# Moving decode, set-up and the last block's projections in a two-layer hybrid decoder step

## The chip, the core and the metric

The kernel runs on one core of one Trainium2 chip. The time is device microseconds of that core for one whole execution: the prompt of 2048 tokens and eight sample tokens through two layers. Three runs are shown, and a profile of one execution.

## What is computed

Each layer normalises its input, makes one projection of width 3332 and feeds four token mixers of width 256, whose outputs, each through its own gate, are concatenated and projected back to 1024:

```python
hn = rms_norm(x, norm_w)
proj = hn @ w_in            # r_q r_k r_v r_g | g_q g_f g_i g_g | s_u s_g | m_z m_xbc m_dt
o_ret  = head_rms(retention(rq, rk, rv)) * silu(r_g)              # "A"
o_hgrn = head_rms(gated_recurrence(hq, hk, hv, log_f)) * silu(g_g) # "H"
gy = gelu(s5_scan(s_u) + s5_D * s_u)                               # "S"
o_s5 = gy * sigmoid(gy @ s5_glu_w + s5_glu_b) * silu(s_g)
o_m2 = rms(ssd(conv(m_xbc), m_dt) * silu(m_z))                     # "M"
x = x + concat(o_ret, o_hgrn, o_s5, o_m2) @ w_out
```

The same layers are applied to the prompt (states start at zero) and to the eight sample tokens (states are given); all new states are outputs. A final rms_norm ends both streams. All is float32.

## The kernel before

**Tiling.** The prompt goes in eight blocks of 512 tokens, four to a layer, in order; `blocks[0..3]` are layer 0, `blocks[4..7]` layer 1. In this document *step i* is the i-th pass of the main loop over blocks. A block's normalised input is held transposed in eight tiles `hn`, each as a rounded value and its remainder, so that each projection takes three matmul passes (L620, L625, L687). Weights come in slices `wr`, are split into `wh` on ScalarE and VectorE (L607/608, L680/681) and used at once. A projection is a Python generator that yields after every slice: 8 yields for a wide one (`gemm_wide`, 512 columns), 4 for a narrow one (`gemm`, 256 columns). Block i has A and H projections (16 yields each), M (12) and S (8), and an output projection (16 in two halves of 512 columns).

**Mixers.** `mix_A`, `mix_H`, `mix_S` and `mix_M` are generators too. `begin` puts one into a lane. After every yield of a projection, `tick` runs at most two mixers one step each (lanes m, s, a, h) and one step of the lanes d, e, f, p (decode and set-up). `yield n` in a mixer asks for n rounds of pause, cut to `most` (1 for the first block's A and H, else 9). `drain` runs named mixers to their end with no projection between. So the order of TensorE's instructions is written out by this code and kept (`manual_schedule` for PE); the other engines and the DMA queue on SP are ordered by the compiler's list scheduler, which follows program order shifted by `high_priority` offsets (set-up is put back by 100, decode by 50, projection weights ahead by 100).

**The main loop before.** Step i runs the A and H projections of block i, drains the mixers of block i-1, begins A and H of block i, runs the output projection of block i-1, then M and S projections with their mixers, and in between prepares the next block's `hn` (L581 to L584). In block 7 the order is: A, H, first half of block 6's output, S, M, second half of block 6's output, block 7's output.

**Set-up and decode.** `s5_setup` makes the S5 tables of a layer from its parameters (exponentials and sines by polynomial on VectorE, table pieces through DRAM: `gpad`, then L517, then `s5c`). Layer 0's is spawned at the start, layer 1's in step 1. `Dec` is the decode of the eight sample tokens: its projections ride on the block's (`dec_pass`, L630 and L694: the raw weights against eight columns), then `mix_A`, `mix_H`, `mix_M`, `mix_S` of `Dec` (L890 to L1070) on VectorE and SP, then its output. It is attached to blocks 0 and 4, the first of each layer.

**Buffers.** Pools have fixed counts: ten `half` tiles (128x512) and ten `big` tiles (128x1024) for all mixers, evictions, set-up and decode; eight `mx` tiles for the mixed outputs of a block. A mixer stores into an `mx` tile (`mix_store`, L722 to L725) only when the previous block's second output half has used it:

```python
def free(self, kt):
    return lambda: self.prev is None or self.prev.used > kt
```

S5's last part (L1458 to L1481) multiplies tables with states, transposes, applies Gelu (L1467), the GLU matmul (L1474), sigmoid (L1476) and the two products L1477 and L1478. Mamba's token tiles need masks from GpSimd (L1561), end in L1597/L1598 and L1637. The heads' post-processing of A and H ends in L736. The last block's output projection (`final` in `out_proj`) drains mixers between its slices:

```python
for g in gens[:2]:
    for k2 in range(3):
        drain(B.st["ahs"[k2]])
        next(g)
        yield
drain(B.st["m"])
```

In this kernel `E('g')`, `E('l')`, `E('s')`, `E('t')` stand for VectorE, `E('m')`, `E('f')`, `E('w')` for GpSimd.

Of the kernel before, what the change touches and what calls it, by code (L numbers as in the profile page):

```python
# [21 lines left out]
P = 128  # L22
D = 1024
KT = 8
# [89 lines left out]
def trunk_kernel(ctx: ExitStack, tc: tile.TileContext, A: dict):  # L114
# [229 lines left out]
    def sincos(sn, cn, hi, lo, shape):  # L344
        n = tmp_c(shape)
        r = tmp_c(shape)
# [19 lines left out]
    def s5_setup(L):  # L366
# [102 lines left out]
        for hf in range(2):  # L469
            yield 2  # L470
            ctz = half([P, 2, 4, 2, 16])
            gtile = half([P, 2, 8, 16])
# [197 lines left out]
    def gemm_wide(lhs, w, c0, evac, dec=None):  # L670
# [4 lines left out]
        def load(kt):  # L675
            with tc.high_priority(offset=WPRI):
                hl = whp.tile([P, 2, 520], F32R, name=nm("wh"), tag="wh")
                raw = wrp.tile([P, 520], F32, name=nm("wr"), tag="wr")
                nc.sync.dma_start(raw[:, 0:512], w[kt * P : (kt + 1) * P, c0 : c0 + 512])
# [5 lines left out]
        def t_pass(kt, tt):  # L685
            for pi, (a, c) in enumerate(((1, 0), (0, 1), (0, 0))):
                T.matmul(banks[tt], lhs[kt][:, a, tt * P : (tt + 1) * P], hls[kt][:, c, 0:512],  # L687
                         start=(kt == 0 and pi == 0), stop=(kt == KT - 1 and pi == 2))

        def dec_pass(kt):  # L690
            if dec is not None and kt % DW == DW - 1:
                for k in range(kt - DW + 1, kt + 1):
                    j = k % 4
                    T.matmul(dbank[32 * j : 32 * j + 8, :], dec[0]()[:, k, :], raws[k][:, 0:512], start=(k < 4), stop=(k >= 4))  # L694
# [43 lines left out]
    class Blk:  # L738
# [48 lines left out]
    class Dec:  # L787
# [209 lines left out]
        def mix_S(self):  # L997
            l, L = self.l, self.L
            gw = load_gw(L)
# [30 lines left out]
            y = half([P, 8, 2, 16])[0:8]  # L1030
# [11 lines left out]
            so = half([P, 2, P])[0:64]  # L1042
# [4 lines left out]
            db = half([P, 2, 256])[0:8]  # L1047
            us = half([P, 2, 256])[0:8]
            nc.sync.dma_start(us[:, 0], self.d["su"])
            nc.sync.dma_start(us[:, 1], self.d["sg"])  # L1050
            nc.sync.dma_start(db[:, 0], A["s5_D"][l].partition_broadcast(8))
            nc.sync.dma_start(db[:, 1], A["s5_glu_b"][l].partition_broadcast(8))
            V.tensor_tensor(db[:, 0], db[:, 0], us[:, 0], ALU.mult)
            V.tensor_tensor(yf, yf, db[:, 0], ALU.add)
# [6 lines left out]
            V.tensor_copy(gT, ps[:, 0:16].rearrange("p (k b) -> p k b", k=2))  # L1061
            yield 4
# [3 lines left out]
            V.tensor_tensor(db[:, 1], db[:, 1], ps[0:8, 0:256], ALU.add)  # L1066
            S.activation(db[:, 1], db[:, 1], AF.Sigmoid)
            V.tensor_tensor(yf, yf, db[:, 1], ALU.mult)
            V.tensor_tensor(yf, yf, us[:, 1], ALU.mult)
# [190 lines left out]
    def mix_H(L, B):  # L1260
# [124 lines left out]
    def mix_S(L, B):  # L1385
# [77 lines left out]
        for th in range(2):  # L1463
            ps = mbank()
            for t in range(4):
                T.transpose(ps[:, t * P : (t + 1) * P], Y[:, 7 - 4 * th - t, :], ident)
            S.activation(gy.rearrange("p h (j t) -> p t h j", t=8)[:, 4 * th : 4 * th + 4], ps.rearrange("p (t h j) -> p t h j", t=4, h=2),  # L1467
                         AF.Gelu_apprx_tanh)
        yield 2
        for mo in range(2):  # L1470
# [6 lines left out]
            E('g').tensor_tensor(sg, sg, B.sg[:, mo, :], ALU.mult)  # L1477
            V.tensor_tensor(sg, sg, gy[:, mo, :], ALU.mult)  # L1478
# [527 lines left out]
```

## Time and profile before

| | us |
|---|---|
| median of 3 runs | 2297.53 (2296.26 to 2297.86) |
| the profiled execution's own time | 2296.06 |
| span in its trace | 2294.3 |
| TensorE matmul busy | 2140.4 (93%) |
| VectorE busy | 1668.9 (73%) |
| ScalarE busy | 1037.3 (45%) |
| GpSimd busy | 236.4 (10%) |

Read the table together with the slices and stretches below: a share over the whole span hides where an engine waits. A busy TensorE may also run at the lower of its two clock levels (the column PEclk: 1.00 is the full level in all of the stretch).

### The profile page before, as it was taken

How to read it: one execution, taken by the hardware profiler on the slowest of the kernel's cores; microseconds unless marked ns; L12 is line 12 of the kernel's file. 1: busy time of each engine (PE TensorE's matmuls, PEld its weight loads, DVE VectorE, ACT ScalarE, POOL GpSimd, SP SyncE). 2: the span in 40 equal slices, each digit the busy share in tenths (PEclk: the TensorE clock that was granted, in tenths of full speed). 3: DMA queues.
4: the chain of work that ended last, by engine and by line, in shares of the span. 5: the costliest groups of instructions: out<-in, count | busy, mean ns of one | idle time of the engine just before them, and what ended most of it. 6: DMA issues, size and time to landing. Idle time of an engine off the chain costs nothing. (4 is left out here: it accounts for less than half of the span.)

```text
span 2294.3 us, 41082 instructions
## 1 busy us (share of the span) xinstructions
PE 2140.4 (93%) x15047; PEld 1732.4 (76%) x15047; DVE 1668.9 (73%) x4625; ACT 1037.3 (45%) x1893; POOL 236.4 (10%) x212
## 2 busy tenths in 40 slices
PE   7988898999999999999999999899999989999967
PEld 6767676778777887779777777676877778778856
DVE  6778885587957876397676798658875787647855
ACT  5334633346442464434543365334545345444423
POOL 1010102001022011101020000200101001110100
PEclk9998899999999999999999999999999999999988
DMA  6322466154533655243434246415454433533342
GB/s 190 91 58 71 155 167 155 50 147 127 168 101 109 159 161 165 68 138 87 146 116 134 82 134 180 145 61 177 116 159 122 127 105 100 163 87 109 121 134 84
DMA packets 265242, 284.94 MB, mean 124 GB/s; under 512 B 88848, under 2 KB 185760, under 8 KB 265040
## 3 DMA queue, kind: packets, MB, share of 16 engines
q1 hardware_dynamic: 265040, 282.31, 41.7%
q8 instruction: 118, 1.93, 0.3%
q14 instruction: 84, 0.69, 0.1%
HBM read 246.05 MB, written 31.99 MB: 121 GB/s over the span
## 5 line engine op out<-in xcount | busy, mean ns | idle before, releaser
L687 PE MATMUL gb<-wh,hn 128*128 128x512 f32 x2208 | 542.0, 401 | 3.7 <-DVE half L1626 3.6
L625 PE MATMUL gb<-hn,wh 128*128 128x512 f32 x1920 | 489.0, 408 | 7.0 <-DVE half L1118 7.0
L687 PEld LDWEIGHTS gb<-wh,hn 128*128 128x128 f32 x2208 | 411.3, 189 | 109.8 <-issue 13.8
L625 PEld LDWEIGHTS gb<-hn,wh 128*128 128x128 f32 x1920 | 361.7, 193 | 98.0 <-issue 11.9
L681 DVE TENSOR_TENSOR wh<-wr,wh 128x512 fp32r<-128x512 f32 x296 | 216.3, 735 | 273.2 <-ACT wh L680 271.7
L680 ACT CAST wh<-wr 128x512 fp32r<-128x512 f32 x296 | 183.4, 620 | 394.1 <-PE gb L687 193.4
L687 PE MATMUL gb<-wh,mx 128*128 128x512 f32 x1344 | 339.3, 405 | 7.4 <-DVE half L1700 6.9
L687 PEld LDWEIGHTS gb<-wh,mx 128*128 128x128 f32 x1344 | 250.0, 191 | 75.6 <-DVE half L1700 11.6
L607 ACT CAST wh<-wr 128x512 fp32r<-128x512 f32 (+1 forms) x248 | 152.2, 619 | 320.1 <-PE gb L625 95.9
L608 DVE TENSOR_TENSOR wh<-wr,wh 128x512 fp32r<-128x512 f32 (+1 forms) x248 | 183.2, 745 | 87.0 <-ACT wh L607 85.8
L620 PE MATMUL gb<-wh,hn 128*128 128x256 f32 (+1 forms) x1728 | 225.2, 291 | 2.1 <-DVE hn L556 1.1
L620 PEld LDWEIGHTS gb<-wh,hn 128*128 128x128 f32 x1728 | 217.6, 196 | 5.6 <-issue 2.6
L1561 POOL TENSOR_TENSOR half<-mats,m_lal 128x512 fp32r<-128x512 f32 x64 | 75.4, 1199 | 820.8 <-DVE m_lal L1555 311.0
L1317 DVE COPY_PREDICATED big<-lvl,mb 64x256 f32<-64x256 int32 x192 | 95.9, 538 | 2.7
L1284 ACT COPY zbH<-big 64x512 f32<-64x512 f32 x112 | 70.8, 632 | 46.7 <-PE mb L1293 39.4
L1499 DVE SCALAR_TENSOR_TENSOR big<-gb,vt,big 128x511 f32<-128x511 f32 (+2 forms) x96 | 71.1, 744 | 3.9 <-ACT big L1497 3.4
L1293 PE MATMUL mb<-zbH,big 128*64 128x64 f32 x1536 | 58.2, 232 | 5.2 <-ACT half L1165 3.5
L1293 PEld LDWEIGHTS mb<-zbH,big 128*64 128x64 f32 x1536 | 51.9, 145 | 14.5 <-issue 7.7
L1275 POOL TENSOR_TENSOR big<-mats,h_dg 128x1024 f32<-128x1024 f32 x16 | 30.6, 1932 | 282.3 <-DVE h_dg L1272 282.3
L1458 PE MATMUL mb<-big,big 128*64 128x128 f32 x512 | 40.7, 304 | 18.2 <-DMA big<-s5c 14.2
L620 PE MATMUL gb<-wh,mx 128*128 128x256 f32 x384 | 51.1, 298 | 4.6 <-DVE mx L1481 4.1
L620 PEld LDWEIGHTS gb<-wh,mx 128*128 128x128 f32 x384 | 50.0, 204 | 6.1 <-DVE mx L1481 4.9
(495 smaller groups left out, 3084.6 us busy)
## 6 DMA issues: line engine op xcount, KB each, us to landing
wr<-in_w_in SPq DMA_DIRECT2D x416, 256.0 KB
wr<-in_w_out SPq DMA_DIRECT2D x128, 256.0 KB
big<-s5c SPq DMA_DIRECT2D x64, 256.0 KB
xn<-xmid SPq DMA_DIRECT2D x32, 512.0 KB
xn<-in_x_prompt SPq DMA_DIRECT2D x24, 512.0 KB
big<-s5c SPq DMA_DIRECT2D x24, 512.0 KB
xmid<-half SPq DMA_DIRECT2D x44, 256.0 KB
half<-xmid SPq DMA_DIRECT2D x44, 256.0 KB
```

Of the source, the lines that this page charges most:

```text
L607: S.copy(hl[:, 0, :, :n], raw[:, :, :n])
L608: V.tensor_tensor(hl[:, 1, :, :n], raw[:, :, :n], hl[:, 0, :, :n].bitcast(F32), ALU.subtract)
L620: T.matmul(o, lhs[2 * ks[ki] + k][:, a, tt * P : (tt + 1) * P], hls[ki][:, c, k, :n], start=(ki == 0 and k == 0 and pi == 0 and tt % per = ...
L625: T.matmul(banks[i], hls[ki][:, a, k, i * P : (i + 1) * P], lhs[2 * ks[ki] + k][:, c, :], start=(ki == 0 and k == 0 and pi == 0), stop=(ki ...
L680: S.copy(hl[:, 0, 0:512], raw[:, 0:512])
L681: V.tensor_tensor(hl[:, 1, 0:512], raw[:, 0:512], hl[:, 0, 0:512].bitcast(F32), ALU.subtract)
L687: T.matmul(banks[tt], lhs[kt][:, a, tt * P : (tt + 1) * P], hls[kt][:, c, 0:512], start=(kt == 0 and pi == 0), stop=(kt == KT - 1 and pi = ...
L1284: S.copy(qz[sl, r, :].rearrange("p (b h) -> p b h", h=h), q[sl].rearrange("p a (b two h) -> p (a b) two h", two=2, h=h)[:, :, 1, :])
L1293: T.matmul(ps[su, j * 64 : (j + 1) * 64], k[:, j // 4, (j % 4) * P + 64 * u : (j % 4) * P + 64 * u + 64], qz[:, :, j * 64 + 32 * u : j * 6 ...
L1317: V.copy_predicated(stv[p][su, :, nu * u : nu * u + nu, :], mv, ps[su, p * 256 : p * 256 + 256].rearrange("p (c b h) -> p c b h", c=8, h=h))
L1499: V.scalar_tensor_tensor(acc[:, 3 - i :], ps[:, : TB - 3 + i], w(i), acc[:, 3 - i :], ALU.mult, ALU.add)
L1561: E('m').tensor_tensor(mms[tt][i].rearrange("p (h t) -> p h t", h=4), tri[:, None, :].to_broadcast([P, 4, P]), lal[:, i, tt, :][:, :, None ...
```

## The change

- Decode rides on the second block of each layer (blocks 1 and 5) in place of the first (0 and 4). Its norm is prepared as a stream in the step before.
- Layer 1's parameters are loaded in step 1 as before, but its S5 set-up waits until the S5 part of layer 0's decode is done, which falls into step 2.
- In block 0, mixer A begins right after the A projection, not after H; `most` is 2 there, not 1.
- Block 7 runs its projections in the order A, H, M, S, with A and H mixers beginning before M, and then the whole output projection of block 6; its own output projection takes the slices in the order A, H, M, S, with S drained last, and loads the final norm's weights after that.
- `used` becomes a set, so that slices may be used in any order.
- Half tiles: set-up and decode use fewer (`cmul` with two temporaries in place of four, one tile for two small ones, GLU weights loaded later); two HGRN level tiles share one.
- S5: the gate is multiplied with the Gelu output once for both halves, before the GLU matmul.

```diff
@@ cmul
-        t1, t2 = tmp_c(shape), tmp_c(shape)
-        V.tensor_tensor(t1, ar, br, ALU.mult)
+        t2 = tmp_c(shape)
+        V.tensor_tensor(outr, ar, br, ALU.mult)
         e.tensor_tensor(t2, ai, bi, ALU.mult)
-        V.tensor_tensor(outr, t1, t2, ALU.subtract)
-        t3, t4 = tmp_c(shape), tmp_c(shape)
+        V.tensor_tensor(outr, outr, t2, ALU.subtract)
+        t3, t4 = outi, tmp_c(shape)
@@ Blk
-        used = 0
+        order = tuple(range(KT))
         def free(self, kt):
-            return lambda: self.prev is None or self.prev.used > kt
+            return lambda: self.prev is None or kt in self.prev.used
@@ mix_H
-            ntot = (half([P, 2, nb]) if l < 3 else small([P, 2, nb], f"h_t{l}", bufs=1))
+            if l == 0:
+                ntot = half([P, 2, nb])
+            elif l < 3:
+                if l == 1:
+                    t12 = half([P, 384])
+                ntot = (t12[:, 0:256] if l == 1 else t12[:, 256:384]).rearrange("p (a b) -> p a b", a=2)
+            else:
+                ntot = small([P, 2, nb], f"h_t{l}", bufs=1)
@@ mix_S
+        E('g').tensor_tensor(B.sg, B.sg, gy, ALU.mult)
         yield 2
         for mo in range(2):
...
-            E('g').tensor_tensor(sg, sg, B.sg[:, mo, :], ALU.mult)
-            V.tensor_tensor(sg, sg, gy[:, mo, :], ALU.mult)
+            V.tensor_tensor(sg, sg, B.sg[:, mo, :], ALU.mult)
@@ out_proj
-        if last:
+        def load_fw():
             for i in range(2):
                 fwb[i] = half()
                 nc.sync.dma_start(fwb[i], A["final_norm_w"][i * 512 : (i + 1) * 512].partition_broadcast(P))
...
         if not final:
+            if last and 1 in parts:
+                load_fw()
             for hf in parts:
-                for k, _ in enumerate(gemm_wide(B.mix, w, hf * 512, evac_wide(hf), dec=B.dec and B.dec.out(hf, last))):
-                    if hf == 1:
-                        B.used = k + 1 if k < 6 else (6 if k == 6 else 8)
+                ks = B.order if hf == 1 else Blk.order
+                for k, _ in enumerate(gemm_wide(B.mix, w, hf * 512, evac_wide(hf), dec=B.dec and B.dec.out(hf, last), ks=ks)):
+                    if hf == 1 and k != 6:
+                        B.used.update(ks[: k + 1])
                     yield
         else:
...
-                gens.append(gemm(B.mix, w, hf * 256, "T", evac(hf), dec=dec, late=hf == 3))
+                gens.append(gemm(B.mix, w, hf * 256, "T", evac(hf), dec=dec, ks=(0, 1, 3, 2), late=hf == 3))
             for g in gens[:2]:
                 for k2 in range(3):
-                    drain(B.st["ahs"[k2]])
+                    drain(B.st["ahm"[k2]])
                     next(g)
                     yield
-            drain(B.st["m"])
+            drain(B.st["s"])
+            load_fw()
@@ begin
-        B.st[ph] = spawn(ph, mixer(ph, B), most=1 if B.prev is None and ph in "ah" else 9)
+        B.st[ph] = spawn(ph, mixer(ph, B), most=2 if B.prev is None and ph in "ah" else 9)
@@ the start
-        B.dec = Dec(layers[0], A["x_sample"].rearrange("b o d -> b (o d)"))
-        ll, dn, ga = load_layer(layers[0]), B.dec.norm(), gemm_A(B.L, B)
+        ll, ga = load_layer(layers[0]), gemm_A(B.L, B)
...
-        next(dn)
-        next(ga)
-        for _ in dn:
-            pass
+        load = setup = None
         setup = spawn("p", s5_setup(layers[0]), SPRI, "s")
@@ the main loop
+            if nxt is None:
+                run(gemm_A(B.L, B))
+                run(gemm_H(B.L, B))
+                drain(*B.prev.st.values())
+                begin("a", B)
+                begin("h", B)
+                run(gemm_M(B.L, B))
+                begin("m", B)
+                run(gemm_S(B.L, B))
+                begin("s", B)
+                finish(B.prev)
+                finish(B)
+                break
             run(ga if i == 0 else gemm_A(B.L, B))
+            if B.prev is None:
+                begin("a", B)
             run(gemm_H(B.L, B))
...
+            if B.b == 0:
+                drain(load)
+                nxt.dec = Dec(B.L, B.prev.dec_dst if B.prev else A["x_sample"].rearrange("b o d -> b (o d)"))
+                prep = spawn("d", nxt.dec.norm(), DPRI, "d")
+            run(gemm_M(B.L, B))
+            begin("m", B)
+            if B.dec:
+                begin_dec(B, "ahm")
+            if B.b == 0:
+                drain(prep)
+            if nxt.l != B.l:
+                drain(load)
...
+            if B.b == 1 and B.l + 1 < DEPTH:
+                load = spawn("p", load_layer(layers[B.l + 1]), SPRI, "s")
+                def after(B):
+                    yield lambda: B.st["ds"].done
+                    yield from s5_setup(layers[B.l + 1])
+                setup = spawn("p", after(B), SPRI, "s")
```

`gemm_wide` takes the order of its slices as `ks`. Not shown: the joined tiles of `s5_setup` and of the decode's `mix_S`.

## Rows read from the trace of the kernel before

**Rows 1.** The page's 40 equal slices: busy tenths of TensorE and its granted clock.
```profile
PE   7988898999999999999999999899999989999967
...
PEclk9998899999999999999999999999999999999988
```

**Rows 2.** Stretches: from:to, length, busy us of each engine, PEclk, DMA share, GB/s.
```profile
15.20:130.00 114.80, 109.22 (x612) 85.66 (x611) 80.38 (x302) 52.15 (x114) 8.54 (x9) 0.97 0.39 115
130.00:278.20 148.20, 122.76 (x1042) 100.24 (x1040) 127.24 (x361) 68.56 (x116) 17.88 (x16) 0.87 0.30 89
278.20:566.50 288.30, 270.16 (x1902) 215.51 (x1902) 212.57 (x553) 123.46 (x223) 32.82 (x26) 0.97 0.47 131
566.50:840.90 274.40, 261.97 (x1812) 215.35 (x1810) 213.06 (x652) 124.43 (x221) 37.50 (x34) 0.98 0.50 137
840.90:1098.80 257.90, 253.24 (x1763) 208.20 (x1762) 177.30 (x469) 121.81 (x214) 27.03 (x26) 0.99 0.40 120
1098.80:1383.10 284.30, 273.88 (x1924) 211.20 (x1922) 213.38 (x547) 135.31 (x241) 23.17 (x22) 0.98 0.40 126
1383.10:1663.00 279.90, 265.79 (x1880) 211.72 (x1879) 216.27 (x584) 126.16 (x237) 27.92 (x23) 0.99 0.45 132
1663.00:1926.50 263.50, 253.03 (x1755) 207.24 (x1754) 183.52 (x489) 125.62 (x228) 26.24 (x22) 0.98 0.43 128
...
2039.80:2150.80 111.00, 110.02 (x945) 93.93 (x945) 80.07 (x229) 48.33 (x87) 3.77 (x2) 0.98 0.35 100
2150.80:2251.60 100.80, 73.98 (x542) 60.63 (x540) 67.83 (x197) 34.97 (x66) 13.56 (x10) 0.88 0.42 136
2251.60:2294.30 42.70, 31.46 (x240) 31.12 (x240) 20.74 (x57) 14.53 (x46) 0.00 (x0) 0.82 0.21 69
```

The busy columns are PE, PEld, DVE, ACT and POOL, each with its count of instructions. Steps 1 to 6 of the main loop are the stretches that begin at 278.20, 566.50, 840.90, 1098.80, 1383.10 and 1663.00.

**Rows 3.** TensorE's timeline at the start: start us, us, instruction, [idle before <-releaser].
```profile
26.12 3.11 PE L620 MATMUL gb<-wh,hn 128*128 128x256 f32 x24
33.72 1.02 PE L800 MATMUL mb<-mats,big 8*128 8x8 f32 x8 [4.49 <-DVE big L812]
34.67 5.20 PE L620 MATMUL gb<-wh,hn 128*128 128x256 f32 x24
```

**Rows 4.** Waits of TensorE, 130 to 278.2 us: us in total, times, longest.
```profile
PE mb L722 <- DVE half L736: 9.0, 2, 4.9
```

**Rows 5.** Waits of TensorE in step 1, 278.2 to 566.5 us.
```profile
PE mb L1458 <- DMA big<-s5c: 8.6, 3, 4.0
PE mb L1474 <- DMA half<-in_s_glu_w: 2.4, 1, 2.4
```

**Rows 6.** Timeline of SP's DMA issues in step 1.
```profile
330.70 5.02 SPq L517 DMA_DIRECT2D big<-gpad  x4
...
338.72 7.49 SPq L1014 DMA_DIRECT2D big<-pd_su  x11
...
349.57 2.16 SPq L517 DMA_DIRECT2D big<-gpad  x3
```

**Rows 7.** Waits of TensorE in the last block, 2039.8 to 2251.6 us.
```profile
PE mb L1608 <- DVE half L1597: 8.4, 1, 8.4
PE mb L722 <- DVE half L1637: 4.8, 1, 4.8
PE mb L1608 <- DVE half L1700: 4.1, 1, 4.1
PE gb L620 <- DVE mx L1481: 4.1, 1, 4.1
PE mb L1474 <- ACT big L1467: 2.2, 1, 2.2
...
PE mb L1466 <- ACT big L1459: 0.7, 1, 0.7
```

**Rows 8.** VectorE's timeline in the last block: S5's two products.
```profile
2222.95 1.29 DVE L1477 TENSOR_TENSOR half<-half,big 128x512 f32<-128x512 f32 x2 [11.67 <-ACT half L1476]
2224.16 1.29 DVE L1478 TENSOR_TENSOR half<-half,big 128x512 f32<-128x512 f32 x2
```

**Rows 9.** GpSimd's timeline in the last block: one of Mamba's masks.
```profile
2196.06 1.15 POOL L1561 TENSOR_TENSOR half<-mats,m_lal 128x512 fp32r<-128x512 f32 x1 [17.89 <-DVE rs L231]
```

More of the change, by code (lines that the diff above doesn't have):

```diff
@@ L470, in s5_setup @@
             yield 2
-            ctz = half([P, 2, 4, 2, 16])
-            gtile = half([P, 2, 8, 16])
+            cg = half()
+            ctz = cg[:, 0:256].rearrange("p (a q r c) -> p a q r c", a=2, q=4, r=2)
+            gtile = cg[:, 256:512].rearrange("p (z g c) -> p z g c", z=2, g=8)
             G.memset(ctz, 0.0)
@@ L668, in gemm, with gemm_wide @@
             yield
-    def gemm_wide(lhs, w, c0, evac, dec=None):
+    def gemm_wide(lhs, w, c0, evac, dec=None, ks=tuple(range(KT))):
         banks = [gps.tile([P, 512], F32, name=nm("gb"), tag="gb") for _ in range(4)]
@@ L693, in dec_pass @@
                     j = k % 4
-                    T.matmul(dbank[32 * j : 32 * j + 8, :], dec[0]()[:, k, :], raws[k][:, 0:512], start=(k < 4), stop=(k >= 4))
+                    T.matmul(dbank[32 * j : 32 * j + 8, :], dec[0]()[:, ks[k], :], raws[k][:, 0:512], start=(k < 4), stop=(k >= 4))
         for kt in range(KT - 2):
@@ L998, in mix_S @@
             l, L = self.l, self.L
-            gw = load_gw(L)
             si = half([P, 2, P])[0:64]
@@ L1029, in mix_S @@
             yield 8
-            y = half([P, 8, 2, 16])[0:8]
+            yso = half()
+            y = yso[0:8, 0:256].rearrange("b (q r c) -> b q r c", q=8, r=2)
             for r in range(2):
@@ L1046, in mix_S @@
             yf = y.rearrange("b q r c -> b (q r c)")
[L1047 to L1054, printed above, removed]
+            ud = half([P, 2, 256])[0:8]
+            nc.sync.dma_start(ud[:, 0], self.d["su"])
+            nc.sync.dma_start(ud[:, 1], A["s5_D"][l].partition_broadcast(8))
+            V.tensor_tensor(ud[:, 1], ud[:, 1], ud[:, 0], ALU.mult)
+            V.tensor_tensor(yf, yf, ud[:, 1], ALU.add)
             S.activation(yf, yf, AF.Gelu_apprx_tanh)
@@ L1862, in trunk_kernel @@
         blocks.append(B)
-        B.hn, B.st = [], {}
+        B.hn, B.st, B.used = [], {}, set()
     def mixer(ph, B):
@@ L1943, in trunk_kernel @@
                 convc = zeroed(small([P, 3, 4], "convc"))
-            if nxt is not None:
-                rows, rs = norm_stats(nxt.b, srcdst(nxt.l)[0])
-                if nxt.l != B.l:
-                    drain(setup)
-                    nxt.dec = Dec(layers[nxt.l], B.dec_dst)
-                    prep = spawn("d", nxt.dec.norm(), DPRI, "d")
-                run(gemm_M(B.L, B))
-                begin("m", B)
-                if B.dec:
-                    begin_dec(B, "ahm")
-                if nxt.l != B.l:
-                    drain(prep)
-                norm = norm_block(layers[nxt.l], rows, rs, nxt.hn)
-                run(gemm_S(B.L, B), lambda n: next(norm, 0) if n >= 3 else None)
-                for _ in norm:
-                    pass
-                begin("s", B)
-                if B.dec:
-                    begin_dec(B, "s")
-                if B.b == 1 and B.l + 1 < DEPTH:
-                    drain(setup)
-                    setup = spawn("p", then(load_layer(layers[B.l + 1]), s5_setup(layers[B.l + 1])), SPRI, "s")
-                nxt.dec_dst = B.dec.dst if B.dec else getattr(B, "dec_dst", None)
-            else:
-                run(gemm_S(B.L, B))
-                begin("s", B)
-                run(gemm_M(B.L, B))
-                begin("m", B)
-                finish(B.prev, parts=(1,))
-                finish(B)
@@ new lines, in trunk_kernel @@
+            rows, rs = norm_stats(nxt.b, srcdst(nxt.l)[0])
+            if B.b == 0:
[10 more added lines that the diff above has]
+                drain(load)
@@ new lines, in trunk_kernel @@
+            norm = norm_block(layers[nxt.l], rows, rs, nxt.hn)
+            run(gemm_S(B.L, B), lambda n: next(norm, 0) if n >= 3 else None)
+            for _ in norm:
+                pass
+            begin("s", B)
+            if B.dec:
+                begin_dec(B, "s")
+            if B.b == 1 and B.l + 1 < DEPTH:
[4 more added lines that the diff above has]
+                setup = spawn("p", after(B), SPRI, "s")
```

26 lines of the change are left out of this document (14 added, 12 removed).

## The prediction

> **What bounds the kernel now.** I read the page's slices first, then the stretches by loop step, then who TensorE waits for in each bad stretch. The slices show TensorE at nine tenths nearly everywhere, with two weak ends: the first seven and the last two [rows 1]. The stretches put numbers to that [rows 2]. For each I take as *lost* its idle time (length less PE busy) plus (1 - granted clock) x length. The second part is right only where TensorE works during the low level, so idle alone is the lower bound. Rows 3 show the cost of the low level: twenty-four 128x256 matmuls took 5.20 us right after a wait of 4.49 us and 3.11 us before it, the clock standing at its lower level of 1.2 GHz instead of 2.4 for a part of them.
>
> Lost, from rows 2: start to 130 us 5.6 + 3.4 = 9; 130 to 278 us (block 0: retention and HGRN mixers beside the Mamba and S5 projections) 25.4 + 19.3 = 45; step 1 (278 to 567) 18.1 + 8.6 = 27; step 2 12.4 + 5.5 = 18; step 3 4.7 + 2.6 = 7; step 4 10.4 + 5.7 = 16; step 5 14.1 + 2.8 = 17; step 6 10.5 + 5.3 = 16; the last block 1.0 + 2.2 = 3 (2040 to 2151) and 26.8 + 12.1 = 39 (2151 to 2252); then 11 us behind the last matmul (42.7 less 31.5). Step 3 shows that the program can run with 7 lost in 258 us. So the limit is TensorE's own work, and what a reordering can give or take is the lost time.
>
> **What the change moves, part by part.** TensorE's work is the same before and after: decode passes and set-up matmuls only change block. So I cost each stretch by its lost time.
>
> *Start.* Layer 0's decode norm no longer stands before the fourth step of the first projection. Its transposes waited 4.49 us and the matmuls behind lost 2.1 more [rows 3]. How much of this the last normalised columns would have cost anyway no row shows: between nothing and all. The retention mixer now also falls into this stretch, under the HGRN projection, where VectorE is at 70% (80.38 of 114.80 [rows 2]). Term: -5 us (-8 to 0).
>
> *Block 0, 130 to 278 us.* VectorE is busy 127 of 148 us [rows 2]; TensorE's longest waits are for the heads' post-processing [rows 4]. The whole decode leaves, and the retention mixer is gone one projection earlier; the HGRN mixer goes at half the pace (a step every two rounds, not every round); the set-up stays. A layer's decode holds VectorE for (213.38 + 216.27) - (177.30 + 183.52) = 69 us and TensorE for (273.88 + 265.79) - (253.24 + 253.03) = 33, steps 4 and 5 against 3 and 6 [rows 2], so VectorE gains the more. The nearest row for a block with such an extra load is step 4 (16 lost in 284 us, so 8 in 148), the lower end; the upper is 40, where only waits on decode tiles go. I take 19, nearer the lower, since three causes of the wait go and one stays. Term: -26 us (-36 to -5).
>
> *Step 1.* TensorE waited 8.6 us here for the S5 tables and 2.4 for the GLU weights [rows 5]. On SP's queue the decode's loads of its S5 input (eleven of them 7.49 us) stood between the pieces that build the table [rows 6]. They now come a block later, so the chain should land sooner. But step 1 takes the decode's projection passes and the start of its mixers, as step 4 has them now with 16 lost, and the end of block 0's HGRN mixer. From 27 I go to 19. Term: -8 us (-14 to +1).
>
> *Steps 2 and 3.* Step 2 gets most decode mixers (as step 5 today: 17) and, once the S5 decode is done, layer 1's set-up. Today's step 2 already carries that set-up, at 18 lost against 7 in step 3 and 16 in step 6; so set-up costs up to 11, and half of it slides into step 3. Terms: step 2 +5 (-2 to +12), step 3 +4 (0 to +10). Here the decode's gain may be handed back.
>
> *Steps 4 to 6.* Decode goes from steps 4 and 5 to 5 and 6: the same rows in another order, 16 + 17 + 16. Term: 0 (-5 to +5). The fewer half tiles of set-up and decode and the shared level tile take no instruction away; S5's product with the gate becomes one 128x1024 in place of two 128x512. All this is hidden behind TensorE's steps, except in the last block.
>
> *Last block.* I count rounds (one after each projection step; up to two mixers step in one) from the start of retention and HGRN. Before: output half 0 to round 8, S5 projection to 16, Mamba projection to 28, output half 1 to 36, then the last output. Mamba needs some 19 rounds after its projection and gets 8, so it pays its chain in the open: 8.4 + 4.8 + 4.1 us [rows 7], plus half speed. After: Mamba projection to 12, S5 to 20, both halves to 36. Mamba's last token tile is done at round 26 and its stores at 36 and 37, when block 6 has given its mix tiles free; these three waits lose their cause. S5 needs some 26 rounds and gets 22, counting the six interleaved steps of the last output; the rest is drained in the open. What stands there today is 0.7 (copy), 2.2 (Gelu) and 4.1 (gate to mix tile) [rows 7]; the gate chain loses one of two products, 1.29 us for the pair [rows 8]. I price S5's end at 6 idle and 3 at half speed: 9.
>
> Against it stands crowding. Retention and HGRN now share rounds 1 to 12 with Mamba's convolution; Mamba and S5 share 21 to 36 with sixteen output steps and their evictions. And half tiles get short: the finished outputs of retention and HGRN (two each) wait for block 6's second half (rounds 29 to 32), Mamba holds two, the final norm's weights two: eight of ten, while Mamba's masks alone want two. Today's trace has such a case: the masks start after 17.89 us of idle GpSimd [rows 9], and the wait of 8.4 us follows. No row shows the new crowd; lower end 6 (step 3's rate over 212 us), upper 45 (five waits like the longest, some half speed behind them). I take 21, nearer the lower, since most rounds have other TensorE work to run. So 9 + 21 = 30 of today's 42 lost. Term: -12 us (-27 to +12). The last output columns and the 11 us behind them stay.
>
> **The clock.** The parts of lost time that come from the clock add up to 67 us, 2.9% of the span. The Trainium skill, "TensorE: Matmul & The Clock Gate" (What's actually happening), says that for modelling, the slow start of the clock is under 1% of a typical span. By that only idle would count, and the sum below would be about -25 instead of -42, still inside the forecast; the trace does not agree, by the 2.9%.
>
> **Sum.** -5 - 26 - 8 + 5 + 4 + 0 - 12 = -42 us. The profiled execution took 2296.06 us (span 2294.3), so 2254. It was 1.5 us under the runs' median of 2297.53; for the median I say 2256.
>
> **Rivals.** A measurement here tells 0.2%, 4.6 us, from no change.
>
> - *Set-up alone keeps block 0 full*, and the decode's bill is paid again: start -5, block 0 -10, step 1 0, steps 2 and 3 +13, tail -8, so -10 and 2287. For it: set-up by itself costs up to 11 us in step 2. Against it: the two decode steps lose 33 us together, only 10 more than steps 3 and 6. Chance 0.13. The Trainium skill's "TensorE: Matmul & The Clock Gate" (Architectural detail) says that VectorE and ScalarE are strictly first in, first out; long decode instructions would then hold up mixer ones in any block, which the 33 us bear out in part.
> - *No change that can be measured*, 2293 to 2302: waits only change their names. Nothing speaks for an even balance. Chance 0.05.
> - *Slower: half tiles in the last block*, rounds 18 to 36. If each of Mamba's four token tiles and the four evictions of output half 0 waits like today's longest (8.4 idle, 1.7 at half speed), that is 81 us beside S5's 9: the tail loses 90 instead of 42, +48 against -30 from the rest, 2316. It decides from seven such waits on (68 us where I take 21). Against it: there are projection steps between them. Chance 0.09.
> - *More than forecast*: every term but steps 2 to 6 at its better end, -8 - 36 - 14 - 27 = -85, 2213; half the way there is 2234. Chance 0.07.
> - *Forecast*, 2235 to 2276: 0.66; the rest up to 2293 is the first rival's.
>
> The range 2230 to 2292 leaves out about 0.05 below and 0.14 above; the terms' ends added in squares, 21 us below and 35 above, reach from 2235 to 2291. Faster 0.66 + 0.13 + 0.07 = 0.86; same 0.05; slower 0.09.
>
> **What would show it.** Right: no wait at L800 in the start; block 0's stretch up to block 1's first projection shorter by 25 to 45 us, without the 4 to 5 us waits on head post-processing; L1458 waiting under 4 us in step 1; steps 1 and 2 near 280 us each; in the last block no wait on Mamba's tiles above 3 us, and one gap of some 3 us each for Gelu and gate. Wrong: a granted clock under 0.9 that stays in block 0 without the decode (then set-up or mixer latency was the cause); step 2 or 3 above 290 us (set-up meets decode); repeated waits on L1561's masks or on evictions (L1700) in the last block (half tiles).

## The result, and the profile after

The changed kernel takes 2261.05 us (median of 4 runs, 2259.51 to 2272.76) against 2296.9 us before (median of 4, 2294.07 to 2297.86): a ratio over all runs of 0.9857, 95% interval 0.9823 to 0.9891 (the two medians alone give 0.984). The forecast was 2256 (2230 to 2292). The sum held, partly by luck: its largest term (block 0) brought more than its range, in good part for a reason that was not priced, another (step 2) cost more than its range, and the two misses cancel.

The profiled execution of the changed kernel was the longest of its four, 11.7 us above their median (2272.76, span 2271.0). The fourth experiment is the same kernel again (profiled 2256.93, span 2255.1); where sizes matter I give both.

The stretches after, by loop step as in [rows 2], columns as there. The steps now begin at 15.4, 222.4, 515.2, 813.7, 1076.8, 1332.8, 1622.3 and 1910.9 us:

```profile
15.20:130.00 114.80, 108.64 (x670) 91.43 (x669) 87.55 (x327) 54.11 (x114) 11.10 (x13) 0.97 0.46 131
130.00:222.40 92.40, 87.47 (x733) 76.84 (x732) 76.48 (x213) 51.16 (x90) 16.07 (x15) 0.98 0.36 99
222.40:515.20 292.80, 278.59 (x2013) 216.12 (x2013) 222.61 (x589) 132.35 (x238) 28.73 (x23) 0.98 0.44 128
515.20:813.70 298.50, 276.06 (x1910) 220.22 (x1910) 244.33 (x722) 125.18 (x228) 38.46 (x32) 0.96 0.42 124
813.70:1076.80 263.10, 255.71 (x1779) 210.19 (x1778) 181.61 (x466) 121.83 (x214) 30.55 (x28) 0.99 0.48 135
1076.80:1332.80 256.00, 252.06 (x1767) 207.19 (x1765) 178.07 (x470) 121.44 (x214) 27.21 (x23) 0.99 0.41 122
1332.80:1622.30 289.50, 274.72 (x1923) 212.97 (x1921) 215.59 (x577) 138.29 (x255) 25.26 (x20) 0.98 0.42 132
1622.30:1910.90 288.60, 271.35 (x1878) 216.34 (x1878) 216.44 (x584) 126.04 (x237) 27.84 (x23) 0.96 0.42 126
1910.90:2022.60 111.70, 109.36 (x632) 86.87 (x631) 68.13 (x153) 53.52 (x95) 14.10 (x13) 1.00 0.40 118
2022.60:2112.00 89.40, 83.35 (x734) 72.24 (x732) 69.15 (x202) 38.62 (x66) 9.96 (x7) 0.96 0.25 67
2112.00:2223.00 111.00, 98.34 (x746) 81.07 (x746) 75.09 (x217) 43.20 (x85) 6.79 (x5) 0.92 0.53 170
2223.00:2271.00 48.00, 34.24 (x247) 31.18 (x245) 23.26 (x62) 17.14 (x48) 0.00 (x0) 0.86 0.19 61
```

*Lost* is counted as in the prediction: length less PE busy, plus (1 - granted clock) x length. For block 0's tail that is 92.40 - 87.47 + 0.02 x 92.40 = 6.8, where [rows 2] gave 45. The last block and its end lose 2.3 + 9.6 + 21.5 + 20.5 = 54, where before it was 65: 4.5 from 1926.5 to 2039.8 us (113.30 long, 111.06 busy, clock 0.98), the 3 and 39 of the prediction, and 42.7 - 31.46 + 0.18 x 42.7 = 19 behind them [rows 2].

| part | term | after | same kernel again |
|---|---|---|---|
| start, 15 to 130 | -5 | +1 | -1 |
| block 0, from 130 | -26 | -38 | -40 |
| step 1 | -8 | -7 | -7 |
| step 2 | +5 | +16 | +13 |
| step 3 | +4 | +3 | +4 |
| steps 4 to 6 | 0 | +7 | -3 |
| last block and end | -12 | -11 | -11 |
| sum | -42 | -29 | -45 |
| span less 2294.3 | | -23 | -39 |

Block 0 lies beyond its range (-36 to -5), step 2 beyond its own (-2 to +12), and the start brought nothing.

TensorE's waits in steps 0, 1 and 2 of the changed kernel. Lines behind the edits have moved by up to 19: L1465 is the y matmul (L1458 before), L1474 Gelu (L1467), L1482 the GLU matmul (L1474), L1488 S5's mix tile (L1481), L1709 the output eviction (L1700), L1615 Mamba's token tile (L1608).

```profile
PE gb L625 <- ACT big L1150: 3.7, 1, 3.7
...
PE mb L722 <- DVE half L736: 4.8, 1, 4.8
...
PE mb L1202 <- DVE half L1176: 5.4, 1, 5.4
PE mb L1465 <- DMA big<-s5c: 3.5, 1, 3.5
```

The 4 to 5 us waits for the heads (L722 behind L736, [rows 4]) are gone from step 0, and so is the stall at L800. But one such wait now stands in step 1 (4.8 us, above) and one in step 5 (4.7 us), where the decode rides; before, step 4 had one of 4.2 us and step 1 none. In place of L800 the H projection waits 3.7 us for ScalarE's eviction of the A projection's gate (L1150). That wait (3.7 to 4.8 us) stands in all nine kernels here that start retention early with the decode moved, and in none that starts it late. Step 2 has a new row: retention (L1202) behind VectorE, 5.4 us, while VectorE works off a long row of small set-up instructions. In the last block, 2022.6 to 2231 us:

```profile
PE gb L620 <- DVE convc L1507: 3.6, 1, 3.6
PE mb L1482 <- ACT big L1474: 3.1, 1, 3.1
PE gb L687 <- DVE half L1709: 2.9, 1, 2.9
PE gb L620 <- DVE mx L1488: 2.8, 1, 2.8
PE mb L722 <- DVE half L1709: 2.2, 1, 2.2
```

The long waits of [rows 7] on Mamba's tiles are gone. Gelu and gate wait once each, as foretold; the first row (the wait behind Mamba's convolution, L1507) was not foretold.

### The profile page after: what moved, and what is told of

Read it like the earlier page. It is cut to its first block, busy times and chain, and to the rows that moved or that the text cites. A ratio compares the mean times of both kernels' runs of the same rounds, so it can differ in the third digit from the quotient of the medians.

```text
span 2271.0 us, 41050 instructions
## 1 busy us (share of the span) xinstructions
PE 2133.5 (94%) x15031; PEld 1725.8 (76%) x15031; DVE 1666.2 (73%) x4614; ACT 1031.1 (45%) x1888; POOL 239.8 (11%) x212
## 5 line engine op out<-in xcount | busy, mean ns | idle before, releaser
L625 PE MATMUL gb<-hn,wh 128*128 128x512 f32 x1920 | 483.5, 405 | 14.3 <-DVE half L1118 5.4
L687 PEld LDWEIGHTS gb<-wh,hn 128*128 128x128 f32 x2208 | 413.2, 189 | 109.2 <-issue 10.7
L687 PE MATMUL gb<-wh,mx 128*128 128x512 f32 x1344 | 345.0, 410 | 12.2 <-DVE half L1709 10.8
L687 PEld LDWEIGHTS gb<-wh,mx 128*128 128x128 f32 x1344 | 254.4, 194 | 82.0 <-DVE half L1709 17.5
L608 DVE TENSOR_TENSOR wh<-wr,wh 128x512 fp32r<-128x512 f32 (+1 forms) x248 | 186.4, 758 | 73.4 <-ACT wh L607 72.4
L1465 PE MATMUL mb<-big,big 128*64 128x128 f32 x512 | 40.5, 303 | 14.7 <-DMA big<-s5c 14.7
L1120 POOL TENSOR_TENSOR half<-half,half 128x256 f32<-128x256 f32 x32 | 32.3, 1010 | 199.9 <-DVE half L1118 178.5
```

What stands on the lines that cost most here:

```text
L608: V.tensor_tensor(hl[:, 1, :, :n], raw[:, :, :n], hl[:, 0, :, :n].bitcast(F32), ALU.subtract)
L625: T.matmul(banks[i], hls[ki][:, a, k, i * P : (i + 1) * P], lhs[2 * ks[ki] + k][:, c, :], start=(ki == 0 and k == 0 and pi == 0), stop=(ki ...
L687: T.matmul(banks[tt], lhs[ks[kt]][:, a, tt * P : (tt + 1) * P], hls[kt][:, c, 0:512], start=(kt == 0 and pi == 0), stop=(kt == KT - 1 and ...
```

## The experiments

All ratios are to the kernel before, run beside each experiment on the same chip. The *pair* below is the length of steps 0 and 1 together: a slower pace pushes mixer work out of step 0 into step 1, so step 0 alone misleads. Before, the pair is 551.3 us (263.0 + 288.3). Step lengths are each from one execution; the two of the changed kernel differ by up to 5 us in a step.

**1. Decode and set-up moved, last block as before.**

```diff
-                drain(*B.prev.st.values())
-                begin("a", B)
-                begin("h", B)
+                finish(B.prev, ("a", B), ("h", B), parts=(0,))
+                run(gemm_S(B.L, B))
+                begin("s", B)
                 run(gemm_M(B.L, B))
                 begin("m", B)
-                run(gemm_S(B.L, B))
-                begin("s", B)
-                finish(B.prev)
+                finish(B.prev, parts=(1,))
                 finish(B)
...
```

Not shown: the last output takes its slices and drains its mixers as before, and loads the final norm's weights where it did.

> The changed kernel with the last block's order of before (S5 projection ahead of Mamba's, block 6's second output half between the mixers): only decode and set-up move. By the prediction's sum this is its -42 us without the last block's -12: a ratio to before of 0.987 (2267 us); with the last-block figure read from the two traces (lost time 65 us before, 54 after) it is also 11 us longer than the changed kernel. Rival A, the reorder of the last block brings nothing of its own: as fast as the changed kernel, 0.984. Rival B, the whole gain is the last block's: as before, 1.000.

0.9869 (0.9849 to 0.9888), against 0.985 (0.9831 to 0.987) for the changed kernel beside it. The two longest waits on Mamba's tiles are back in its last block, in the sizes of [rows 7], a third is 2.4 us:

```profile
PE mb L1615 <- DVE half L1604: 8.6, 1, 8.6
PE mb L722 <- DVE half L1644: 4.8, 1, 4.8
```

Its last step takes 364.4 us, 4.3 more than the changed kernel's and 3.4 less than before. So the whole gain is not the last block's (rival B falls); the difference between the two ratios, 0.0019, is inside the intervals, so the size comes from the next one.

**2. The new last block alone.** The changed kernel with `B.dec` on blocks 0 and 4, the set-up spawned as before, retention after HGRN's projection, `most=1`. S5's single product with the gate and the fewer half tiles stay as changed.

> The other half: the changed kernel with decode and set-up where they were before (blocks 0 and 4; set-up beside block 0 and from block 1), and retention started after HGRN's projection; the new order of the last block stays. Theory: the last block alone, 8 to 12 us faster than before, 0.995 to 0.9965, with block 0 (15.2 to its successor's first projection) at 263 us as before. Rival: the last block gains only because of something the moved decode leaves free: 0.999 to 1.001.

0.996 (0.9942 to 0.9977), 9 us: the theory. The last step is 357.5 us against 367.8 before. Its pair is 547.1, 4 us under before's:

```profile
15.20:281.20 266.00, 231.57 (x1652) 184.97 (x1650) 206.06 (x665) 118.59 (x229) 28.68 (x26) 0.92 0.34 101
281.20:562.30 281.10, 268.63 (x1902) 214.90 (x1902) 210.49 (x550) 123.26 (x222) 33.26 (x26) 0.98 0.48 133
```

**3. Late retention at the old pace**, decode and set-up moved.

```diff
-            if B.prev is None:
-                begin("a", B)
             run(gemm_H(B.L, B))
...
+                begin("a", B)
                 begin("h", B)
...
-        ... most=2 if B.prev is None and ph in "ah" else 9)
+        ... most=1 if B.prev is None and ph in "ah" else 9)
```

> The changed kernel, but block 0's retention mixer starts after HGRN's projection and both mixers keep the pace of before (a step each round); decode and set-up as changed. Theory: block 0 was full because of the decode; without it the late start costs 0 to 8 us (2261 to 2269), and block 0 stays under 220 us. Rival: the early start of retention made room in block 0, and block 0 is again 15 to 40 us longer (2276 to 2300).

0.993 (0.991 to 0.995): the theory falls. The decode has left, yet the waits for the heads are there, one of 8.0 us, and the clock stands at 0.93 (the first stretch is step 0, the second step 1; below them waits of step 0):

```profile
15.50:244.80 229.30, 205.57 (x1494) 176.81 (x1492) 180.75 (x582) 106.21 (x205) 30.77 (x28) 0.93 0.37 104
244.80:532.40 287.60, 273.56 (x1922) 212.14 (x1921) 210.40 (x545) 129.90 (x235) 29.00 (x22) 0.98 0.45 131
...
PE mb L722 <- DVE half L736: 13.4, 2, 8.0
```

Up to 130 us TensorE is busy 113.03 of 114.50 us at the full clock; the loss lies behind, at a granted clock of 0.87, the figure of before [rows 2]:

```profile
130.00:244.80 114.80, 92.54 (x830) 80.69 (x828) 95.29 (x274) 49.34 (x85) 17.18 (x17) 0.87 0.24 68
```

Much of what leaves the pair comes back in step 2: the pair is 30 us shorter than in experiment 2 (547.1 to 516.9), step 2 26 us longer, since decode and set-up now stand there. Step 2 of experiment 2, then of this one:

```profile
562.30:834.60 272.30, 261.01 (x1811) 214.90 (x1810) 212.89 (x651) 124.47 (x221) 38.31 (x34) 0.97 0.49 138
532.40:830.50 298.10, 275.09 (x1911) 219.46 (x1910) 243.99 (x722) 125.27 (x228) 36.68 (x32) 0.96 0.42 123
```

**4. The changed kernel again.**

> The changed kernel once more, on the chip of the other three: a ratio to before of 0.982 to 0.987. Its profiled execution was the slowest of its four runs by 11 us; steps 2 and 6 (298.5 and 288.6 us) held 11.9 and 11.5 us of lost clock. If that belonged to that one execution, a second profile shows these steps at 286 to 292 and 277 to 283 us; if it belongs to the kernel, the same waits (S5's tables from DMA, retention's rotated tiles) stand in it again with the low clock behind them.

0.985 (0.9831 to 0.987). Steps 0 to 3:

```profile
15.20:220.20 205.00, 193.53 (x1401) 166.49 (x1399) 163.76 (x539) 104.71 (x202) 27.25 (x27) 0.99 0.41 118
220.20:512.90 292.70, 278.51 (x2012) 216.33 (x2012) 222.65 (x589) 132.66 (x238) 28.64 (x23) 0.98 0.43 128
...
512.90:808.40 295.50, 273.40 (x1911) 218.47 (x1910) 244.45 (x722) 125.43 (x228) 37.71 (x32) 0.97 0.42 125
808.40:1071.50 263.10, 256.75 (x1781) 211.21 (x1779) 181.04 (x466) 121.59 (x214) 30.55 (x28) 0.98 0.48 135
```

Step 2 is 295.5 us, step 6 283.5: step 2's bill belongs to the kernel. Steps 5 and 6 were 5 us longer each in the other execution, with the same waits and more low clock.

**5. Early retention at the old pace.** Only `most=2` back to `most=1`.

> The changed kernel with only the pace of block 0's retention and HGRN mixers put back (at most one round between their steps instead of two); retention still starts after the first projection. The stretch from the first projection of block 0 to the first of block 1 was 263 us before, 229 with late start and old pace, 205 to 207 in the changed kernel. Theory: what counts is the early start; 205 to 212 here, as fast as the changed kernel (0.985, up to 0.988). Rival: the slower pace is what keeps TensorE fed; 222 to 229 here, 0.992 to 0.995.

0.9967 (0.9955 to 0.998): the rival, and beyond it. An early start without the pace is worse than a late one. Step 0 and its waits:

```profile
15.60:256.60 241.00, 211.14 (x1494) 180.59 (x1492) 182.14 (x582) 107.36 (x208) 32.76 (x28) 0.92 0.36 101
...
PE mb L722 <- DVE half L736: 8.3, 1, 8.3
PE gb L625 <- ACT big L1150: 4.5, 1, 4.5
```

**6. Decode in block 0, early retention, new pace.** As 2, but `begin("a")` before `gemm_H` and `most=2`.

> The fourth corner: decode in block 0 and in block 4 as before, set-up of layer 1 from block 1 as before, new last block, but block 0's retention starts after the first projection with the new pace. Theory: decode (34 us, 263 to 229) and late retention (23 us, 229 to 206) are separate loads of the same block, so the early start alone gives the stretch of block 0 some 240 us, and the whole 0.986. Rival: with the decode in it VectorE is too full for the early start to help; 255 to 266 us, 0.994 to 0.997.

0.9966 (0.9954 to 0.9979). Step 0 is 241.9 us, as the theory had it, but the whole is the rival's: step 1 is 307.7, 26.6 more than in 2, with one wait of 6.5 and one of 6.9 us. What pace and early start together give with the decode in place is handed back a step later; neither of the two had said that.

```profile
16.20:258.10 241.90, 217.96 (x1559) 173.12 (x1557) 188.45 (x612) 114.16 (x222) 25.91 (x25) 0.96 0.37 105
258.10:565.80 307.70, 281.14 (x1994) 224.23 (x1994) 226.60 (x602) 126.35 (x227) 32.45 (x27) 0.96 0.45 126
```

**7. Layer 1's set-up held for step 3.**

```diff
-                    yield lambda: B.st["ds"].done
+                    yield lambda: B.st["ds"].done and "s" in blocks[2].st
```

> The changed kernel with layer 1's S5 set-up held back until block 2's S5 mixer has been started, so it runs in step 3 (7 to 12 us lost) instead of step 2 (31 to 34 lost). Theory: step 2's bill comes from set-up meeting the decode; step 2 falls from 295 to 280 to 284, step 3 rises from 263 to at most 272, in all 4 to 8 us faster than the changed kernel (0.981 to 0.983). Rival: the bill is the decode's second step by itself (step 6 has no set-up and lost 24 to 29), and set-up only takes its own work along: step 2 285 to 288, step 3 271 to 275, the whole unchanged (0.985).

0.9868 (0.9849 to 0.9887); the changed kernel was not run beside it. Step 2 falls to 279.2 us, below the theory's range; step 3 rises to 285.5, above the rival's. Together 564.7, where the changed kernel has 558.6 (experiment 4). A single wait takes it:

```profile
515.60:794.80 279.20, 267.94 (x1880) 213.68 (x1880) 208.28 (x553) 123.11 (x222) 28.00 (x23) 0.98 0.42 124
794.80:1080.30 285.50, 262.03 (x1809) 215.30 (x1808) 217.54 (x635) 126.74 (x222) 38.53 (x37) 0.96 0.47 132
...
PE mb L1615 <- DVE half L1602: 16.6, 1, 16.6
```

**8. Layer 1's decode left in block 4.** `nxt.dec` is set at block 0 for layer 0 and at each change of layer.

> The changed kernel with only layer 0's decode moved; layer 1's decode stays in block 4. The prediction's term for steps 4 to 6 is 0. Theory: that term is right, steps 4 to 6 together 824 us +-5 in either order, and the whole as the changed kernel (0.985). Rival: the second decode step is dearer in its new place (24 to 29 us lost in step 6 against 17 in step 5 of before), so leaving it gives 6 to 10 us, 0.981 to 0.983.

0.9876 (0.9857 to 0.9894); steps 4 to 6 together 825.9 us (823.5 in experiment 4, 827.7 before). The rival falls: leaving it gains nothing. The term 0 was right.

**9. Late retention, new pace.** As 3, with `most=2`.

> The changed kernel, but block 0's retention starts after HGRN's projection as before; the new pace (up to two rounds between the mixers' steps) stays. This is the missing corner: late and old pace took 229 us for the stretch of block 0 and 0.993 in all, early and old pace 241 us and 0.997, early and new pace 205 us and 0.985. Theory (formed after the fifth experiment): the pace alone decides, since at one round between steps TensorE comes to a mixer's next matmul before VectorE has its input; 200 to 215 us here, 0.985 to 0.988. Rival: start and pace work only together, 222 to 232 us, 0.992 to 0.995.

0.9858 (0.9831 to 0.9886), step 0 208.3 us: the pace alone, as the theory had it.

```profile
15.30:223.60 208.30, 194.71 (x1373) 167.08 (x1371) 170.27 (x537) 103.52 (x201) 27.95 (x27) 0.97 0.41 116
223.60:518.50 294.90, 282.39 (x2040) 219.38 (x2040) 220.39 (x592) 133.77 (x241) 28.30 (x23) 0.97 0.43 128
```

**10. Set-up after block 2's Mamba mixer.** As 7, with `blocks[2].st["m"].done` in the condition.

> The changed kernel with layer 1's set-up held until block 2's Mamba mixer is done (in step 3). With set-up started when block 2's S5 mixer was (the seventh experiment), step 2 fell to 279 us, but one wait of 16.6 us at a Mamba matmul and 17 us of low clock behind it made step 3 285. Theory: set-up's first piece is one unbroken run of VectorE work, so what it costs depends on which mixer step stands behind it; with no Mamba step in flight that wait goes, step 2 stays at 279 to 283, step 3 is 264 to 272, in all 0.979 to 0.982. Rival: it hits the next mixer instead (S5 of block 2 or retention of block 3), again one wait of 5 us or more, step 3 275 to 285, 0.984 to 0.987.

0.9862 (0.9834 to 0.9891): the rival. Step 3 is 285.3 us; the blow falls on the next in line, the eviction of the A projection's sums (its rotation, L1118), for which the H projection waits, and then on S5's tables. Step 3 and its waits:

```profile
800.80:1086.10 285.30, 262.51 (x1810) 214.99 (x1809) 218.35 (x635) 122.56 (x219) 36.55 (x37) 0.96 0.47 132
...
PE gb L625 <- DVE half L1118: 10.6, 1, 10.6
PE mb L1465 <- DMA big<-s5c: 7.2, 1, 7.2
```

**11. S5's second tables from GpSimd's queue.**

```diff
-                nc.sync.dma_start(tq[:, hb], s5c...
+                (nc.gpsimd if qh else nc.sync).dma_start(tq[:, hb], s5c...
```

(and the same for `cq`).

> The changed kernel with the loads of S5's second half of tables (four per block) issued by GpSimd instead of SP, where they stand behind three weight loads that wait for a free buffer. Those matmuls waited 3.2 to 3.6 us in steps 2, 3 and 6 of the changed kernel, with 3 to 7 us of low clock behind each. Theory: the queue is what delays the tables; the three waits go, 8 to 15 us in all, 0.979 to 0.982. Rival: the transfer or the tables' free buffers set the time, the waits stay at 3 us, 0.985.

0.9902 (0.9877 to 0.9927): the forecast falls. Its fastest run (2266.98 us) is slower than the slowest of experiment 9 beside it (2265.68). GpSimd issues in order too, here at 598.2 us behind the rotations it had to do, 0.5 us for each load, and the loads land 4.5 us after (median of the four). So they were issued no earlier: 18.7 us behind the block's first table load (579.46), where SP's came 17.6 us behind it in experiment 4 (574.06 and 591.68). Whether an earlier issue would end the waits is therefore not tested. The waits for tables grow from 12.2 us in all (experiment 4) to 20.5. Two rows of this run, from GpSimd's timeline and from the waits:

```profile
598.20 0.58 POOL L1454 DMA_DIRECT2D big<-s5c  x1
...
PE mb L1465 <- DMA big<-s5c: 20.5, 12, 4.6
```

**12. Set-up in pieces.** As 10, with `if l: yield` at seven places of set-up's first piece and one in each half.

> As the tenth experiment (layer 1's set-up waits for block 2's Mamba mixer), but layer 1's set-up gives way seven times more in its first piece and once in each later half, so that its VectorE work comes in short runs with a round between them. Whole, that piece kept VectorE for some 20 us, and whatever mixer step or projection eviction stood behind it waited 17 us (16.6 in the seventh experiment, 10.6 + 7.2 in the tenth). Theory: it is the unbroken run that costs; in step 3 no wait is longer than 5 us, step 2 stays at 279 to 283, step 3 is 264 to 271, the whole 0.977 to 0.981, faster than the changed kernel. Rival: VectorE's time is what costs, however it is cut; step 3 stays at 280 or more, 0.985.

0.9874 (0.9851 to 0.9898). The wait of 10.6 us at the evictions is gone, one of 7.3 us for tables stays, and step 3 is 277.1: between the two, and the whole is the rival's. Cut or whole, set-up costs its step 14 to 22 us over the 263.1 of experiment 4 (277.1, 285.3, 285.5), of which 5 to 6 are TensorE's own work for it (262.0 to 263.0 busy against 256.75). None of these versions beats the changed kernel.

```profile
795.00:1072.10 277.10, 262.99 (x1811) 217.13 (x1809) 219.02 (x636) 125.33 (x221) 36.88 (x37) 0.97 0.44 127
```

## Why the prediction was right, and where it was not

**Luck in the sum.** Block 0 gave 12 to 14 us more than its term of -26, step 2 cost 8 to 11 more than its +5, and the start gave 4 to 6 less than its -5. That these come to 2261 beside a forecast of 2256 is luck. What the prediction argued for the first block, the decode's leaving, is experiment 3, and that kernel takes 2278 us.

Steps 0 and 1 in the six corners that were run, the new last block in each of them (lost time by the prediction's formula, in step 0 to 130 us and from there):

| experiment | decode in block 0 | retention | pace | step 0 | lost to 130, from 130 | pair | ratio |
|---|---|---|---|---|---|---|---|
| 2 | yes | late | old | 266.0 | 9, 47 | 547.1 | 0.996 |
| 6 | yes | early | new | 241.9 | 13, 21 | 549.6 | 0.9966 |
| 3 | no | late | old | 229.3 | 1, 37 | 516.9 | 0.993 |
| 5 | no | early | old | 241.0 | 12, 36 | 528.5 | 0.9967 |
| 9 | no | late | new | 208.3 | 2, 18 | 503.2 | 0.9858 |
| 4 | no | early | new | 205.0 | 8, 5 | 497.7 | 0.985 |

"No" in the second column moves the rest of decode and set-up too, so a pair compares only with pairs of the same entry there. The order 2, 3, 9, 4 adds one edit at a time.

**Block 0: size too small, reason half right.** The failing step is "three causes of the wait go and one stays", priced as one with the decode in front ("VectorE gains the more"). From 130 us on, the decode's leaving takes only 10 of the lost time (47 to 37), the pace 20 (37.2 to 17.6), and the early start 13 with the pace (18 to 5). Without the pace the early start takes next to nothing there (37 to 36) and costs 11 before 130 us. In the whole, moving decode and set-up is worth 0.996 less 0.993, some 7 us (the intervals just overlap); the pace behind it 0.993 less 0.9858, some 16 us (different chips, intervals well apart); the early start nothing that can be told with the pace (0.9858 and 0.985) and a loss of 8 us without it; and pace and early start together, with the decode in place, nothing (0.9966). The order of TensorE's work is written out, so a mixer step one round after the other brings TensorE to a matmul whose input VectorE has not finished: in experiment 3 it came to L722 at 210.4 us and went on at 218.7 (the last section shows where 3.4 us of that come from). With two rounds another slice of a projection stands between, there 24 matmuls of 128x256, 3.1 us. The prediction mentions the halved pace once and gives it no number. Its own sign for "set-up or mixer latency was the cause" was a granted clock under 0.9 that stays in block 0 without the decode, and experiment 3 shows it: 0.87 from 130 us on. Experiment 9 tells the two apart: set-up stays where it was, and the pace alone brings 0.94 there. The first rival (set-up keeps block 0 full without the decode) thus had the size nearer than the forecast did (2278 us against its 2287), but not the cause. It lost only because the change also moves the pace.

**Start: no gain.** The stall of [rows 3] is gone, and it was worth its price: with the decode moved and retention late, experiments 3 and 9 lose 1.5 and 1.6 us up to 130 us, where [rows 2] has 9. But early retention puts 3.7 us at the H projection and the low clock behind it. In experiment 9, without the early start, the H projection follows at 65.8 us, not 70.1. The failing step is that the prediction saw retention come into this stretch and gave it no price; with the pace, the early start earns this back from 130 us on.

```profile
15.30:130.00 114.70, 113.09 (x613) 95.59 (x613) 85.05 (x303) 55.42 (x119) 15.68 (x15) 1.00 0.50 141
```

**Step 1: right.** 20 lost for a forecast of 19; no wait on tables or GLU weights in step 1 of the changed kernel above 1 us, where [rows 5] had 8.6 and 2.4. A wait for the heads of 4.8 us, which step 1 did not have before, has come with the decode.

**Step 2: too small.** The failing step is "half of it slides into step 3". Set-up stayed in step 2: 34 lost (31 in experiment 4) for a forecast of 23. The rows of before add up: 7 for a step with neither (step 3), some 10 more for decode (step 5) and 11 more for set-up (step 2) make 28 [rows 2]. Experiment 7 shows step 2 without set-up: 279.2 - 267.94 + 0.02 x 279.2 = 17 lost, what decode alone cost in step 5 before. So the two did not make each other worse by much; they were simply both there, and moving one moves its bill. That set-up's long first piece is what costs was only half shown: cutting it took 8 us off step 3 (285.3 to 277.1, one execution each), not the rest, and the whole became no faster (0.9862 and 0.9874).

**Steps 4 to 6: right**, +7 and -3 in two executions (the +7 is outside the term's 5, with more low clock), and experiment 8.

**Last block: right in size and mechanism.** -12 foretold, -11 by lost time, 9 us alone (experiment 2); the part priced at 30 lost 31; the Mamba waits go with the new order and return with the old (experiment 1). Half tiles did not run out: evictions (L1709) wait 2.9 and 2.2 us, once each.

**The marks I set.** Right: L800, the heads' waits in step 0, step 1's tables, Mamba's tiles, Gelu and gate. Wrong: block 0 became 56 us shorter, not 25 to 45, and steps 1 and 2 came to 293 and 298, not 280. I had costed lost time alone, and forgot in the marks that TensorE's decode work moves as well: PE busy fell from 109.2 + 122.8 to 108.6 + 87.5 in step 0, and rose in steps 1 and 2 by 8 and 14 us [rows 2]. "Step 2 above 290 us" was my mark for set-up meeting decode, and it was met. One sum of the prediction is wrong: its rival "more than forecast" leaves out the +9 of steps 2 and 3, with which -85 is -76 and 2213 is 2222.

**The clock.** Its part of the lost time fell from 19.3 to 1.9 us in block 0, as well as the idle (25.4 to 4.9). Step 0 was granted 0.93 and 0.92 in experiments 3 and 5, where TensorE waited 8 us at a time, and 0.97 and 0.99 in experiments 9 and 4, where it did not. Over the whole span idle fell from 142.5 to 120.9 us (before and experiment 4, summed over the stretches), 22 us, and the span by 39, so idle alone tells little over half of the gain. Summed in the same way, the clock's part is 77 us before and 55 in experiment 4, 3.4% and 2.4% of the span. The Trainium skill's rule from "TensorE: Matmul & The Clock Gate" (What's actually happening) is that for modelling the slow start stays under 1% of a span; the trace does not agree. *Lost* counts some of this twice, since the clock is also low while TensorE waits: in experiment 7, from 812 to 836 us, TensorE works 6.24 of 24 us at a granted clock of 0.74.

**Open.** What still costs step 3 its 14 us when set-up comes in pieces was not settled: one wait of 7.3 us for S5's tables stands there, and whether VectorE's load or SP's queue delays them was not told apart. Finer pieces for layer 0 were not tried. The pace alone and the early start alone were not run with the decode in place, and S5's product with the gate and the saved half tiles were never run by themselves.

## What to carry to other kernels

Where one engine's order is written out by hand, look first at how many of its other instructions stand between a producer's step and its consumer; spacing can be worth more than taking work away, and may show its worth only once the work is gone. Cost a moved piece twice, in lost time and in the busy time that moves with it, and follow it into the next step, where a gain in the first is often given back. When a change carries several edits into one stretch, give each its own number, or say that the sum cannot tell them apart.

## What the runs showed of the hardware

A 128x8 VectorE instruction with both inputs in SBUF takes 0.16 us, but up to 1.03 us while GpSimd works on Mamba's masks (four masks from 211.02 to 216.63 us). Experiment 3, GpSimd first, then VectorE inside and behind that stretch:

```profile
211.02 5.61 POOL L1568 TENSOR_TENSOR half<-mats,m_lal 128x512 fp32r<-128x512 f32 x4 [12.22 <-DVE m_lal L1562]
...
210.87 0.16 DVE L231 TENSOR_TENSOR rs<-hp_rs 128x8 f32<-128x8 f32 x1
...
211.55 1.03 DVE L232 TENSOR_TENSOR rs<-rs,rs 128x8 f32<-128x8 f32 x1
212.50 0.68 DVE L302 TENSOR_TENSOR big<-pwr,bb 128x512 f32<-128x512 f32 x1
...
217.60 0.16 DVE L232 TENSOR_TENSOR rs<-rs,rs 128x8 f32<-128x8 f32 x1
```

Four instructions of the heads' chain (L231 to L233) took 0.96 to 1.03 us there, 3.4 us more than at their usual 0.16, and the wait of 8.0 us at L722 stands behind that chain. The Trainium skill, "SBUF — State Buffer" (Who interferes with whom), says that a VectorE instruction with two SBUF inputs contends with a GpSimd instruction that reads SBUF, and that whichever comes second is blocked for the whole of the other. The trace agrees, and shows both sides blocked in turn. Three VectorE instructions of 128x512 (L608, L302, L309) stand between the small ones and take their usual 0.68 us, while the masks take 5.61 / 4 = 1.4 us each, where [rows 9] has 1.15 for one; the small ones, at about 1 us, wait out most of a mask each.
